# Loading the first indices ahead of x on one DMA queue, in a max-unpool kernel

## Chip, cores, metric

One Trainium2 chip, one core of it. The time is the device time of one execution in microseconds; medians are given with the lowest and highest run.

## The reference

Each value of `x` goes to one of the four places of a 2x2 block of the output, chosen by an index from 0 to 3; the other three places are zero.

```python
def setup_inputs():
    batch, channels, h, w = 16, 64, 32, 32
    return {"x": np.random.randn(batch, channels, h, w).astype(np.float32),
            "indices": np.random.randint(0, 4, (batch, channels, h, w)).astype(np.int32),
            "kernel_size": 2}

# for every b, c, i, j:
idx = indices[b, c, i, j]
output[b, c, 2 * i + idx // 2, 2 * j + idx % 2] = x[b, c, i, j]
```

On the device `x` has 4 MiB, the indices, which arrive as 64-bit integers, 8 MiB, and the output 16 MiB.

## The kernel before

There are 1024 images of 32x32, eight on each of 128 partitions. Everything is loaded by three transfers on the Sync queue: all of x, the indices of the first three images (`FIRST = 3`), the other five. VectorE writes, for each of the four places, `(index == place) * x`, two images per operation, or one at the border between the two loads of indices. Two images make a group, and each of the four groups is stored by one transfer of 4 MiB. The fourth group reuses the first output buffer. A semaphore is a counter on which an engine waits: each load raises its own by 16, one for each of the 16 DMA engines that carry it, and has landed with the last of these increments.

```python
    cut = FIRST * 2 * N
    with Program(nc) as program:        # puts the loads at the head of the Sync queue
        program.first(nc.sync.dma_start(out=x_t, in_=x_v).then_inc(x_in, 16))
        for half, part in enumerate((slice(0, cut), slice(cut, None))):
            program.first(
                nc.sync.dma_start(out=idx_t[:, part], in_=idx_v[:, part]).then_inc(
                    idx_in[half], 16))

        nc.vector.wait_ge(x_in, 16).then_inc(x_in, -16)
        for t in range(T):
            g, k = t // G, t % G
            if t in (0, FIRST):
                half = int(t == FIRST)
                nc.vector.wait_ge(idx_in[half], 16).then_inc(idx_in[half], -16)
            # ... (n is 1 or 2 images)
            for pidx in range(4):
                op = nc.vector.scalar_tensor_tensor(
                    out=o_c[:, k : k + n, :, pidx // 2, :, pidx % 2],
                    in0=idx_c[:, t : t + n], scalar=pidx, in1=x_c[:, t : t + n],
                    op0=mybir.AluOpType.is_equal, op1=mybir.AluOpType.mult)
            if k + n == G:
                op.then_inc(made, 1)

        for g in range(NG):
            nc.sync.wait_ge(made, g + 1)
            nc.sync.dma_start(out=out_v[g], in_=out_t[g]).then_inc(
                stored if g else stored_0, 16)
        # ... (wait for the last stores)
```

Of the kernel before, what the change touches and what calls it, by code (L numbers as in the profile page):

```python
# [1 line left out]

# [4 lines left out]

P = 128
F32 = mybir.dt.float32
I32 = mybir.dt.int32  # L10


class Program:



    def __init__(self, nc):
        self.nc = nc
        self.block = nc.main_func.blocks[0]
        self.kernel_block = nc.cur_bb.bb.name  # L20
        self.moved = 0

    def __enter__(self):
        ins = self.block.instructions
        self.branches = [i for i in ins if "Branch" in type(i).__name__]
        n = len(ins) - len(self.branches)
        assert all("Branch" in type(ins[k]).__name__ for k in range(n, len(ins)))
        del ins[n:]
        self.nc.switch_bb(self.block.name, parent=None)
        self.symbolic = self.nc._always_lower_symbolic_ap  # L30
        self.nc._always_lower_symbolic_ap = False
        return self

    def first(self, made):
        ins = self.block.instructions
        assert ins[len(ins) - 1].name == made.ins.name
        moved = ins.pop()
        at = next(k for k, i in enumerate(ins) if i.engine == moved.engine)
        ins.insert(at + self.moved, moved)
        self.moved += 1  # L40

    def last(self, made):


        def move(nc):
            ins = self.block.instructions
            at = next(k for k, i in enumerate(ins) if i.name == made.ins.name)
            nc.main_func.blocks[-1].instructions.append(ins.pop(at))

        self.nc.at_finalize(move)  # L50

    def __exit__(self, kind, *_):
        self.nc._always_lower_symbolic_ap = self.symbolic
        if kind is None:
            for b in self.branches:
                self.block.instructions.append(b)
            self.nc.switch_bb(self.kernel_block, parent=None)


@with_exitstack  # L60
def kernel(
    ctx: ExitStack,
    tc: tile.TileContext,
    x: bass.AP,
    indices: bass.AP,
    kernel_size: bass.AP,
    out: bass.AP,
):
    nc = tc.nc
    assert kernel_size == 2  # L70

    B, C, H, W = x.shape
    n_img = B * C
    T = n_img // P
    assert T * P == n_img and C % T == 0

    G = 2
    NG = T // G
    FIRST = 3
    N = H * W  # L80
    x_v = x.rearrange("b (ch t) h w -> (b ch) (t h w)", t=T)
    idx_v = indices.rearrange("b (ch t) h w -> (b ch) (t h w)", t=T).bitcast(I32)
    out_v = out.rearrange("b (ch g t) oh ow -> g (b ch) (t oh ow)", g=NG, t=G)

    x_t = nc.alloc_sbuf_tensor("x_t", [P, T * N], F32).ap()
    idx_t = nc.alloc_sbuf_tensor("idx_t", [P, T * 2 * N], I32).ap()
    out_t = [
        nc.alloc_sbuf_tensor(f"out_t{g}", [P, G * 4 * N], F32).ap()
        for g in range(NG - 1)
    ]  # L90
    out_t.append(out_t[0])

    x_in = nc.alloc_semaphore("x_in")
    idx_in = [nc.alloc_semaphore(f"idx_in{g}") for g in range(2)]
    made = nc.alloc_semaphore("made")
    stored_0 = nc.alloc_semaphore("stored_0")
    stored = nc.alloc_semaphore("stored")

    x_c = x_t.rearrange("p (t i j) -> p t i j", t=T, j=W)
    idx_c = idx_t.rearrange("p (t i j two) -> p t i j two", t=T, j=W, two=2)[  # L100
        :, :, :, :, 0
    ]
    cut = FIRST * 2 * N

    with Program(nc) as program:
        program.first(nc.sync.dma_start(out=x_t, in_=x_v).then_inc(x_in, 16))
        for half, part in enumerate((slice(0, cut), slice(cut, None))):
            program.first(
                nc.sync.dma_start(out=idx_t[:, part], in_=idx_v[:, part]).then_inc(
                    idx_in[half], 16  # L110
                )
            )

        nc.vector.wait_ge(x_in, 16).then_inc(x_in, -16)
        for t in range(T):
# [5 lines that stand above are left out]
            if k == 1 and t != FIRST:  # L121
                continue
            n = 1 if k == 1 or t + 1 == FIRST else 2
            if g == NG - 1:
                nc.vector.wait_ge(stored_0, 16).then_inc(stored_0, -16)
            o_c = out_t[g].rearrange(
                "p (m i two j wo) -> p m i two j wo", m=G, two=2, wo=2, j=W
# [4 lines that stand above are left out]
                    in0=idx_c[:, t : t + n],  # L132
                    scalar=pidx,
                    in1=x_c[:, t : t + n],
                    op0=mybir.AluOpType.is_equal,
                    op1=mybir.AluOpType.mult,
# [7 lines that stand above are left out]
                stored if g else stored_0, 16  # L144
            )
        nc.sync.sem_inc(made, -NG)
        program.last(
            nc.sync.wait_ge(stored, 16 * (NG - 1)).then_inc(stored, -16 * (NG - 1))
        )


# [1 line left out]
_INS = ['x', 'indices', 'kernel_size']  # L153
_OUTS = [((16, 64, 64, 64), 'float32')]

_NUMBERS = {'kernel_size': 2}


# [26 lines left out]
```

## Time and profile before

| | before |
|---|---|
| median of the first three runs | 71.57 us (71.49 to 71.67) |
| span of the profiled run | 70.5 us |
| VectorE | 35.6 us busy, from 19.81 to 55.40 without a gap |
| DMA queue | 97.4% of 16 engines' span |
| landings | x 12.4, first indices 19.6, other indices 31.8 us |

In the profile DVE is VectorE, POOL is GpSimd, PE is TensorE and SP is the Sync engine; a name with q, such as SPq, is the engine's own instruction queue. The stores and loads are issued on SPq and carried by the DMA engines. A wait is put down to the semaphore instruction that held it, so "DVEq L119" is VectorE's own queue waiting at line 119. The prediction below shows the lines.

### The profile page before, as it was taken

How to read it: one execution, taken by the hardware profiler on the slowest of the kernel's cores; microseconds unless marked ns; L12 is line 12 of the kernel's file. 1: busy time of each engine (PE TensorE's matmuls, PEld its weight loads, DVE VectorE, ACT ScalarE, POOL GpSimd, SP SyncE). 2: the span in 40 equal slices, each digit the busy share in tenths (PEclk: the TensorE clock that was granted, in tenths of full speed). 3: DMA queues.
4: the chain of work that ended last, by engine and by line, in shares of the span. 5: the costliest groups of instructions: out<-in, count | busy, mean ns of one | idle time of the engine just before them, and what ended most of it. 6: DMA issues, size and time to landing. Idle time of an engine off the chain costs nothing.

```text
span 70.5 us, 72 instructions
## 1 busy us (share of the span) xinstructions
DVE 35.6 (50%) x20; POOL 0.2 (0%) x4
## 2 busy tenths in 40 slices
DVE  0000000000079999999999999999999400000000
POOL 1000000000000000000000000000000000000000
DMA  9779798899988999969899997979798999979790
GB/s 260 316 316 558 335 558 344 376 432 446 595 372 372 395 511 535 418 298 521 372 428 465 409 483 335 539 316 558 335 521 372 446 446 409 483 335 539 316 558 37
DMA packets 1008, 29.36 MB, mean 416 GB/s; under 512 B 112, under 2 KB 112, under 8 KB 112
## 3 DMA queue, kind: packets, MB, share of 16 engines
q1 hardware_dynamic: 1008, 29.36, 97.4%
HBM read 12.58 MB, written 16.78 MB: 416 GB/s over the span
## 4 chain that ended last, share of the span: by engine, by line
DVE 46%; DVEq 4%; issue 1%
DVE out_t L130 46%; DVEq L180 4%
## 5 line engine op out<-in xcount | busy, mean ns | idle before, releaser
L130 DVE SCALAR_TENSOR_TENSOR out_t<-idx_t,x_t 128x2048 f32<-128x2048 int32 (+1 forms) x20 | 35.6, 1857 | 19.8 <-DVEq L119 19.8
L166 POOL MEMSET const-uint8-127<- 128x1 uint8 x1 | 0.1, 103 | 0.0
L166 POOL MEMSET const-bfloat16-1.0<- 128x1 bf16 x1 | 0.1, 102 | 0.0
L166 POOL MEMSET const-float32-0.0<- 128x1 f32 x1 | 0.1, 99 | 0.2 <-issue 0.2
L166 POOL MEMSET const-float32-1.0<- 128x1 f32 x1 | 0.1, 99 | 0.0
## 6 DMA issues: line engine op xcount, KB each, us to landing
out_dram<-out_t SPq DMA_DIRECT2D x4, 4096.0 KB, 13.8
idx_t<-in_indices_dram SPq DMA_DIRECT2D x1, 5120.0 KB, 30.9
x_t<-in_x_dram SPq DMA_DIRECT2D x1, 4096.0 KB, 12.4
idx_t<-in_indices_dram SPq DMA_DIRECT2D x1, 3072.0 KB, 19.2
```

Of the source, the lines that this page charges most:

```text
L130: op = nc.vector.scalar_tensor_tensor(out=o_c[:, k : k + n, :, pidx // 2, :, pidx % 2], in0=idx_c[:, t : t + n], scalar=pidx, in1=x_c[:, t ...
L166: nc = _bacc.Bacc("TRN2", target_bir_lowering=False, num_devices=1)
L180: with _tile.TileContext(nc) as tc:
```

## The change

The loads are issued in another order: first indices, x, other indices. The apparent aim is to have the indices that VectorE needs first in place early. The helper that puts loads at the head of the queue also changes its rule, from "count what I moved" to "in front of the queue's first drain", which comes to the same place.

```diff
-        at = next(k for k, i in enumerate(ins) if i.engine == moved.engine)
-        ins.insert(at + self.moved, moved)
-        self.moved += 1
+        at = next(k for k, i in enumerate(ins)
+                  if i.engine == moved.engine and isinstance(i, mybir.InstDrain))
+        ins.insert(at, moved)
 ...
+        program.first(nc.sync.dma_start(out=idx_t[:, :cut], in_=idx_v[:, :cut])
+                      .then_inc(idx_in[0], 16))
         program.first(nc.sync.dma_start(out=x_t, in_=x_v).then_inc(x_in, 16))
-        for half, part in enumerate((slice(0, cut), slice(cut, None))):
-            program.first(nc.sync.dma_start(out=idx_t[:, part], in_=idx_v[:, part])
-                          .then_inc(idx_in[half], 16))
+        program.first(nc.sync.dma_start(out=idx_t[:, cut:], in_=idx_v[:, cut:])
+                      .then_inc(idx_in[1], 16))
```

(Line breaks shortened, the rest unchanged.)

More of the change, by code (lines that the diff above doesn't have):

```diff
@@ L20, in __init__ @@
         self.kernel_block = nc.cur_bb.bb.name
-        self.moved = 0
     def __enter__(self):
@@ L37, in first @@
         moved = ins.pop()
-        at = next(k for k, i in enumerate(ins) if i.engine == moved.engine)
-        ins.insert(at + self.moved, moved)
-        self.moved += 1
+        at = next(
+            k
+            for k, i in enumerate(ins)
+            if i.engine == moved.engine and isinstance(i, mybir.InstDrain)
+        )
+        ins.insert(at, moved)
     def last(self, made):
@@ L105 @@
     with Program(nc) as program:
-        program.first(nc.sync.dma_start(out=x_t, in_=x_v).then_inc(x_in, 16))
-        for half, part in enumerate((slice(0, cut), slice(cut, None))):
-            program.first(
-                nc.sync.dma_start(out=idx_t[:, part], in_=idx_v[:, part]).then_inc(
-                    idx_in[half], 16
-                )
+        program.first(
+            nc.sync.dma_start(out=idx_t[:, :cut], in_=idx_v[:, :cut]).then_inc(
+                idx_in[0], 16
+            )
+        )
+        program.first(nc.sync.dma_start(out=x_t, in_=x_v).then_inc(x_in, 16))
+        program.first(
+            nc.sync.dma_start(out=idx_t[:, cut:], in_=idx_v[:, cut:]).then_inc(
+                idx_in[1], 16
             )
+        )
         nc.vector.wait_ge(x_in, 16).then_inc(x_in, -16)
```

## The prediction

> **What bounds the kernel now.** I read the page's head first (busy shares, slices, queues), then the waits, then the issues with their landings, then the timeline, and last a table of stretches that follows the stages those views gave.
>
> The page's busy shares and its DMA lines:
>
> ```profile
> DVE 35.6 (50%) x20; POOL 0.2 (0%) x4
> ...
> DVE  0000000000079999999999999999999400000000
> ...
> DMA  9779798899988999969899997979798999979790
> ...
> q1 hardware_dynamic: 1008, 29.36, 97.4%
> HBM read 12.58 MB, written 16.78 MB: 416 GB/s over the span
> ```
>
> VectorE, the only engine that computes, works 35.6 of 70.5 us, in one block in the middle. The transfers fill 97.4% of what 16 DMA engines could do in the span, in every slice from the first to the last but one. The page's chain of waits ("DVE 46%") starts at a VectorE wait and puts the rest on VectorE; it doesn't follow transfers, so by itself it would point at the wrong resource.
>
> The waits of VectorE, and of the queue that issues:
>
> ```profile
> DVE out_t L130 <- DVEq L119: 19.8, 1, 19.8
> ...
> SPq L143 <- DVE out_t L130: 52.7, 4, 27.0
> SPq L148 <- SPq L148: 14.0, 1, 14.0
> ```
>
> VectorE waits once, 19.8 us, at line 119, for the first load of the indices; afterwards never. The queue waits for VectorE before each of four stores, and 14.0 us at the end for the last store to land.
>
> The page's issues (the last column is issue to landing), and the timeline:
>
> ```profile
> out_dram<-out_t SPq DMA_DIRECT2D x4, 4096.0 KB, 13.8
> idx_t<-in_indices_dram SPq DMA_DIRECT2D x1, 5120.0 KB, 30.9
> x_t<-in_x_dram SPq DMA_DIRECT2D x1, 4096.0 KB, 12.4
> idx_t<-in_indices_dram SPq DMA_DIRECT2D x1, 3072.0 KB, 19.2
> ...
> 0.00 0.38 SPq L106 DMA_DIRECT2D x_t<-in_x_dram  x1
> ...
> 0.43 0.90 SPq L109 DMA_DIRECT2D idx_t<-in_indices_dram  x2
> 19.81 35.59 DVE L130 SCALAR_TENSOR_TENSOR out_t<-idx_t,x_t 128x2048 f32<-128x2048 int32 x20 [19.81 <-DVEq L119]
> 28.73 27.03 SPq L143 DMA_DIRECT2D out_dram<-out_t  x4
> ```
>
> x lands at 12.4, the first indices at 0.43 + 19.2 = 19.6, the other indices at 0.90 + 30.9 = 31.8. VectorE starts 0.2 after the second landing, runs without a gap from 19.81 to 55.40, and the first store is issued at 28.73, when the last indices still have 3 us to go.
>
> The table of stretches (length; busy time of DVE and POOL; clock; DMA share; GB/s):
>
> ```profile
> 0.00:2.00 2.00, 0.00 (x0) 0.20 (x4) 1.00 0.89 246
> 2.00:4.00 2.00, 0.00 (x0) 0.00 (x0) 1.00 0.64 279
> 4.00:12.00 8.00, 0.00 (x0) 0.00 (x0) 1.00 1.02 439
> 12.00:20.00 8.00, 0.19 (x1) 0.00 (x0) 1.00 1.00 429
> 20.00:31.00 11.00, 11.00 (x7) 0.00 (x0) 1.00 1.03 444
> 31.00:41.00 10.00, 10.00 (x8) 0.00 (x0) 1.00 1.02 439
> ```
>
> From 4 us on the rate is 430 to 440 GB/s whichever tensor moves and whichever way. Only the first 4 us are poorer. The transfers bound the time from end to end; VectorE is hidden behind them, as long as it never lets the queue run dry.
>
> The records of single packets in the trace make this exact. Each engine moves eight packets per transfer, one packet per partition row: 1.213 us for 32 KB (x, stores), 0.912 for 24 KB (first indices), 1.514 for 40 KB (other indices), each next one starting as the one before ends. Chained together, the 56 data packets of every engine have no gap over 0.004 us between any two. The first packets begin between 1.01 and 2.35 us. The engine that begins last also ends last: it starts at 2.35, ends x at 12.02, first indices at 19.30, other indices at 31.39, last store at 70.11. So the end is that engine's start plus 67.76 us of packets, plus 0.39 for the last landing and the end of the span.
>
> **What the Trainium skill says.** "DMA: Bandwidth & Descriptors", section "Where 436 GB/s comes from", gives 16 ports x 256 bits x 850 MHz = 435.2 GB/s as the ceiling of a core's transfers. The trace agrees: 32,768 bytes in 1.213 us on 16 engines is 432 GB/s. The same page, "Queues, rings and completion order", has each DMA engine take its descriptors in ring order, with the semaphore written only after that engine's data. The landings (x, first indices, other indices, in order of issue) agree. And "Why a DMA increments its semaphore by 16 and not by 1" says that only the full 16 means all data has landed; so a wait ends with the slowest of 16 engines. Here the 16 increments of a load are spread over 0.7 us, and VectorE starts after the last. "Perfetto Trace Analysis", section "Summary: the profiler window per engine type", says the interval of such an issue leaves out the movement of data: 0.38 us against 12.4 to landing here. So I judge the loads by landings and packets, not by the 0.38.
>
> **The change part by part.** The comparison of instruction orders shows equal lists on every engine but for one swap: the queue now has first indices, x, other indices, where it had x, first indices, other indices. The new rule for where a load is inserted (before the engine's first drain, not at its first instruction) comes to the same place: in both programs the three loads head the issuing engine's list. No byte, packet, wait, or VectorE instruction is added or removed.
>
> 1. Issue. A load of indices takes 0.425 to 0.432 us to issue, x takes 0.383 (the durations of the issues at lines 109 and 106). With the indices in front, the first packet may come 0.04 us later than its 1.01 now. On the path: +0.04.
>
> 2. First indices and x. In either order the two take 8 x 0.912 + 8 x 1.213 = 17.0 us of each engine. On the last engine they take 19.30 - 2.35 = 16.95, the records overlapping by a few ns. What precedes is start-up: 2.35 us from the first issue to that engine's first packet. On most other engines the first packet begins before 1.3 and takes 1.76 to 2.17 us instead of 1.21; the three that begin at 1.41, 1.81 and 2.35 take 1.54, 1.48 and 1.21, so all first packets end between 2.9 and 3.6, and all later ones take their normal time. That looks like a delay that each engine pays once, not like a rate in proportion to size, so I let it stand with 24 KB in front: +0.00.
>
> 3. The landing that VectorE needs. It needs both loads. Now it waits for x until 12.4 and for the first indices until 19.67 (last of 16 increments). Afterwards the indices land at about 2.35 + 8 x 0.91 + 0.37 = 10.0 (0.37 being the time from the last packet's end to its increment, 19.67 - 19.30) and x, 4,096 KB behind 3,072 KB, at 19.7. The wait that lasts changes its name, not its end. The code waits for x first and indices second, so after the x wait ends, one satisfied wait stands between it and the first operation: 0.02 us of its own, with its dispatch perhaps 0.05 to 0.1. VectorE starts at 19.8 to 19.95 and ends at 55.4 to 55.55, with 35.6 us of work as now.
>
> 4. What a late VectorE costs. The first store is issued at 28.73. From issue to first packet takes about 1.0 us (x: 0.00 to 1.01), so its packets could start at 29.74; the first engine is free at 30.71. The slack is 0.97. If the last engine's first packet comes 2.35 after every issue, not only after the first of all, that engine could start at 31.08 and is free at 31.39: slack 0.31. The next issues, at 37.81, 46.62 and 55.43, meet packets that start at 40.39, 50.07 and 59.75: slacks of 1.6, 2.4 and 3.3. A delay of 0.15 fits in the smallest: +0.00. The reused first output buffer is no obstacle either: its store lands at 41.52, and the last group begins at 46.51.
>
> 5. The rest, other indices and stores, is the same series of packets: 70.11 - 19.30 = 50.8 us.
>
> Sum: 71.57 + 0.04 = 71.61, so 71.6.
>
> **The rivals.** One: VectorE starts earlier, since indices come first. That is the apparent aim of such a change, and it would hold if the first operations needed little of x. Against it: line 119's wait shows VectorE starting after all 7,168 KB have landed, x is still one load with one wait, and even an earlier VectorE could not help, since the stores would queue behind the last indices on engines that are already full. Time: unchanged.
>
> Two: the start-up shrinks with the first packet. If the slow first packets are slow in proportion to size, 24 KB rather than 32 KB saves a quarter of the excess, (2.17 - 1.21) / 4, about 0.25: 71.3. For it: they are by far the slowest packets. Against it: the engine that ends last had no slow packet at all, it only began late; it gains nothing unless it begins earlier.
>
> Three: the start-up grows. Rows of indices lie 64 KB apart in memory, each load of them taking a part; rows of x are contiguous. If cold reads of spread rows are slower, or the last engine is served later behind a longer issue, 0.2 to 0.4 is lost: 71.9. Warm reads speak against it: 24 KB in 0.912 us is 26.9 GB/s for an engine, and x's 1.213 is 27.0.
>
> Four: the queue runs dry before the first store because VectorE is late. By step 4 it takes between 0.31 and 0.97 us of delay before anything is lost; nothing in the change makes more than 0.15. If it did, say 1.5 us late, the time would be 72.1.
>
> **Range and chances.** The three runs before spread from 71.49 to 71.67, about 0.1 either way. Start-up is the one term with an open sign, -0.3 to +0.3. That gives 71.3 to 71.9. Two per cent is 1.43 us, more than the whole start-up loss, and steady transfer can't be shortened without fewer bytes: faster 0.01. A loss of that size would need rival four with at least 1.7 us of delay (0.31 + 1.43): slower 0.02. Within 2%: 0.97.
>
> **What would show it right or wrong.** In the issues, first indices landing near 9 to 10 us and x at about 19 to 20 us after issue, other indices 30.9 as now. In the waits, the 19.8 us of VectorE stays within 0.2, now ended by x's landing. The queue's share stays near 97%, the stretches from 4 us on near 430 to 440 GB/s, and the wait for the last store near 14.0. A DMA share well under 0.9 in a stretch around 30 us would mean that the stores came late; other indices landing over 0.3 away from 31.8 would mean that start-up has changed; a VectorE start far from 19.8 would break step 3; a store or load at a lower steady rate would break step 5, and then the prediction as a whole.

## The result

| | before | changed |
|---|---|---|
| median, six runs each | 71.62 us (71.49 to 71.75) | 71.47 us (71.41 to 71.79) |
| ratio | | 0.9989, 95% interval 0.9968 to 1.0011 |

A ratio is the mean time of one kernel's fast runs over that of the other's in the same rounds, so not quite the ratio of the medians. Within 2%, and inside the predicted 71.3 to 71.9.

The page of the changed kernel, busy shares and transfers:

```profile
DVE 35.6 (51%) x20; POOL 0.2 (0%) x4
...
DMA  8799997979988999869898999989898989999891
...
q1 hardware_dynamic: 1008, 29.36, 97.4%
```

Its issues (KB, then us from issue to landing) and its timeline:

```profile
out_dram<-out_t SPq DMA_DIRECT2D x4, 4096.0 KB, 13.8
idx_t<-in_indices_dram SPq DMA_DIRECT2D x1, 5120.0 KB, 30.8
x_t<-in_x_dram SPq DMA_DIRECT2D x1, 4096.0 KB, 19.0
idx_t<-in_indices_dram SPq DMA_DIRECT2D x1, 3072.0 KB, 9.7
...
0.00 0.38 SPq L110 DMA_DIRECT2D idx_t<-in_indices_dram  x1
...
0.43 0.42 SPq L114 DMA_DIRECT2D x_t<-in_x_dram  x1
...
19.67 35.60 DVE L137 SCALAR_TENSOR_TENSOR out_t<-idx_t,x_t 128x2048 f32<-128x2048 int32 x20 [19.67 <-DVEq L126]
28.60 27.03 SPq L150 DMA_DIRECT2D out_dram<-out_t  x4
```

Look at the landings, not at VectorE: the first indices are there at 9.7 instead of 19.6 us, x at 19.4 instead of 12.4. VectorE needs both and so starts at 19.67 where it started at 19.81. The wait changed its cause and kept its end; the queue's share is the same 97.4%.

The waits of VectorE and the last one of the queue:

```profile
DVE out_t L137 <- DVEq L126: 19.7, 1, 19.7
...
SPq L155 <- SPq L155: 14.1, 1, 14.1
```

"L126" is the wait for the first indices, though they had landed 10 us before: it is the second of two waits in a row, and the first, for x, let it through only at 19.45 (the semaphore instruction at line 121). The view names the wait instruction nearest to the operation, not the late transfer. The landings name it.

### The profile page after: what moved, and what is told of

Its sections match the earlier page's. It is cut to its first block, busy times and chain, and to the rows that moved or that the text cites. A ratio compares the mean times of both kernels' runs of the same rounds, so it can differ in the third digit from the quotient of the medians.

```text
span 70.5 us, 72 instructions
## 1 busy us (share of the span) xinstructions
DVE 35.6 (51%) x20; POOL 0.2 (0%) x4
## 3 DMA queue, kind: packets, MB, share of 16 engines
q1 hardware_dynamic: 1008, 29.36, 97.4%
## 4 chain that ended last, share of the span: by engine, by line
DVE 46%; DVEq 4%; issue 1%
DVE out_t L137 46%; DVEq L187 4%
```

## Experiments

Eleven runs were made, one of them of the changed kernel again; the edits below are edits of the changed kernel. Below, A is the theory of the prediction: the packets on the 16 DMA engines bound the time from end to end. B is the rival that the chain of waits suggests: first load, then VectorE, then last store. C came up after the first four runs. Packets are read from the trace's record of single packets. "Effective start" is worked out for each engine: the start of its first packet after 5 us, less what all its earlier bytes would take at the steady rate. All ratios are to the kernel before, run on the same chip, so a run's gain or loss contains the 0.1 to 0.3 us that the changed order itself saves (see after_again). The jobs ran on different chips, so ratios of different jobs are compared only roughly.

### VectorE earlier: e1_split

```diff
-  load indices 0-2;  x 0-7;  indices 3-7
+  load indices 0-2;  x 0-2;  x 3-7;  indices 3-5;  indices 6-7
   # each with its own semaphore, waited for where it is first needed
```

> x and the indices are split in order of need (indices 0-2, x 0-2, x 3-7, indices 3-5, indices 6-7), same bytes, same queue. Both theories: VectorE needs only 4.7 MB before its first operation, which land at about 2.4 + 10.9 + 0.4 = 13.7 us instead of 19.5, and it then runs its 35.6 us almost without a wait, to about 49.3. Theory A (the engines' packets bound the time end to end): the stores still queue behind the last indices, whose last packet ends near 31.4; time 71.5, plus or minus 0.2, wait for the last store 20 us instead of 14. Theory B (the path is first load, VectorE, last store): 6 us are saved, 65.5.

Measured: 72.79 us (72.64 to 72.91), ratio 1.0144 (1.0115 to 1.0173). VectorE did start 6 us earlier, and the first store was issued at 22.32 instead of 28.60:

```profile
13.40 26.84 DVE L145 SCALAR_TENSOR_TENSOR out_t<-idx_t,x_t 128x2048 f32<-128x2048 int32 x16 [13.40 <-DVEq L130]
22.32 29.60 SPq L158 DMA_DIRECT2D out_dram<-out_t  x4
```

B is dead: 6 us earlier in, nothing gained. But A isn't whole either; it said 71.5, and the kernel lost 1.1 us against before. The packets tell where. All loads ran at their normal pace until 28.5 us. Then the last three packets of each engine (16 KB, normally 0.611 us) took up to 1.28, and the stores began at 31.8 to 32.5 instead of 30.7 to 31.4. From there on everything was steady again.

### Fewer bytes: e2_less and e3_split_less

```diff
-  load indices 3-7                     # e2; in e3 the split loads of e1 without the last
+  load indices 3-5
-  in0=idx_c[:, t : t + n]
+  in0=idx_c[:, t % 6 : t % 6 + n]      # wrong result for images 6 and 7, on purpose
```

> 2.1 MB of indices (images 6 and 7) are not loaded and the last group uses images 0 and 1 again: a wrong result on purpose. VectorE's start and work stay. Theory A counted naively: 2.1 MB at 432 GB/s are 4.85 us, 66.6. Theory A with the slack of my prediction: the loads end near 26.55, but the first store is issued only at 28.6 and its first packets come at 29.6 or later, so only the slack is won, 0.97 us (70.5) if all engines start promptly, down to 0.3 (71.2) if one starts as late as at the start of the program; the engines idle about 3 us before the first store. Theory B: unchanged, 71.5.

> Both of the above: loads split in order of need, and 2.1 MB less (wrong result on purpose). Now VectorE starts at about 13.7, its first group is done by 22.6, before the loads end at about 26.5, so nothing hides the bytes saved. Theory A: 71.5 - 4.85 = 66.6, share of the queue again near 97%. Theory B: as e1, 65.5, with no difference between e1 and e3.

e2: 70.10 us (70.04 to 70.15), ratio 0.9769. A hole opens in the transfers, two slices (of 1.7 us) at zero, while the first store waits for VectorE, issued at 28.44:

```profile
DMA  8699998897999980097978979798797977979793
...
28.44 27.03 SPq L151 DMA_DIRECT2D out_dram<-out_t  x4
```

In the packets each engine idles 3.1 to 3.6 us, and all sixteen begin the store between 29.28 and 29.44, 0.8 to 1.0 us after its issue. So the gain against before was 1.6 us, not the 4.85 of the bytes and not nothing, and more than the 0.3 to 1.0 that I expected: here no engine begins its store late, as some began the first load, so the slack of the engine that ends last is 31.39 - 29.7 = 1.7 us. The cautious branch of the prediction's step 4 (slack 0.31) was wrong.

e3: 67.91 us, ratio 0.9465. Against e1, which differs only in those bytes, that is 72.79 - 67.91 = 4.88 us, and 2.1 MB at 432 GB/s are 4.85. Where nothing hides them, bytes cost what A says. The level is 1.3 us too high for A, as with e1: the last two load packets of each engine (24 KB, normally 0.912) took up to 1.78.

### VectorE later: e4_late and e5_late_small

```diff
+  nc.vector.scalar_tensor_tensor(out=scratch[:, :NN], in0=x_t[:, :NN], scalar=0.0,
+      in1=x_t[:, :NN], op0=is_equal, op1=mult)   # once, before the first operation
   # NN = 2048 in e4, 256 in e5
```

> One extra VectorE operation on 2048 elements into a scratch tile before the first: VectorE is 2.2 us later, all else equal. Theory A: the first store is issued at 30.8, its packets start at about 31.8 on engines that are free between 30.6 and 31.4, so 0.4 to 0.7 us are lost on the engine that ends last (72.0 to 72.2), and up to 1.8 if an engine starts its store late again (73.3). A gap of 0.4 to 1.3 us shows in each engine's packets before the first store and nowhere else. Theory B: the full 2.2 us, 73.7.

> The changed kernel with one dummy VectorE operation on 256 elements, 0.33 us, in front. Theory A with its slack (at least 0.31 us, by e2 and e4 nearer 1 us): no loss, 0.995 to 0.997 of before as the changed kernel, or 0.1 us less where a few last packets no longer meet the first store. Theory B: 0.33 us more than the changed kernel, 1.000 to 1.001 of before.

e4: 72.35 us (72.19 to 72.41), ratio 1.0080 (1.0053 to 1.0107), so 2.2 us of delay cost 0.6 against before; a little above the 72.0 to 72.2 of A, far from B's 73.7. The gap before the first store is 0.51 to 1.05 us in the packets, and no gap elsewhere exceeds 0.03.

e5: 71.54 us, ratio 0.9983 (0.9971 to 0.9994). The delay was 0.35 us (19.50 to 19.85), and nothing is lost to be seen against before. The ratio lies between the 0.995 to 0.997 expected of A and the 1.000 to 1.001 expected of B, and both lie just outside its interval. So this run separates nothing; e4 does that.

### The order again: after_again

> The changed kernel once more, for a sharper ratio to the kernel before on one chip. Theory A (only start-up can differ): ratio between 0.996 and 1.004. A rival with start-up in proportion to the first packet's size: 0.25 us less, ratio 0.9965.

71.47 us (71.39 to 71.60) against 71.79 (71.66 to 71.97), ratio 0.9961 (0.9947 to 0.9975). With the first 0.9989, the change saves something like 0.1 to 0.3 us. That is real on this chip. It fits the rival with start-up in proportion to size (0.9965) as well as A; e7 and e10 below decide that. It isn't VectorE's doing, for 6 us there gained nothing (e1). The span was 70.1 us; the changed kernel's first profile, 70.5, fell on its slowest run (71.79).

### Why the split lost: e8_split_late and e9_early_store

Theory C: a store that stands queued behind a load that is still running slows the end of that load. In e1 the store was queued 9 us before the engines were free; in both original kernels only 2.

```diff
 # e8: e1, and before the first operation
+  three dummy VectorE operations of 2.2 us, into scratch
 # e9: the changed kernel, whole loads, and
-  nc.vector.wait_ge(x_in, 16)          # before the first operation
+  if t == 2: nc.vector.wait_ge(x_in, 16)
-  in1=x_c[:, t : t + n]
+  in1=(x_c if t else idx_c)[:, t : t + n]    # wrong result for the first group, on purpose
```

> The split loads of e1, but three dummy VectorE operations of 2.2 us in front, so that the first store is issued at about 29 us as in the changed kernel and not at 22.3. Theory C (in e1 the last 48 KB per engine of the loads ran at about half rate because a store already stood queued behind them): the loss of 1.1 us goes away, 71.5 to 71.8, and the last 16 KB packets take 0.61 us again. Rival D (five smaller loads cost more than three): 72.8 as e1.

> The changed kernel with its three whole loads, but the first group takes the indices in place of x (a wrong result on purpose), so VectorE starts after the first load, at about 9.8 us, and the first store is issued at about 18.9 while the last load still has 12 us to go. Theory C: the last 40 KB packet or two of each engine slow down as in e1, the time is 0.8 to 1.3 us above the changed kernel, 72.4 to 72.8. Rival D: 71.5, like the changed kernel, for the loads are the same.

e8: 71.55 us (71.54 to 71.62), ratio 0.9972. The split alone costs nothing. e9: 72.93 us (72.89 to 73.05), ratio 1.0164, a little beyond the expected range. It has the loads of the changed kernel and the loss of e1. The first store's issue in e8, then in e9, where VectorE's later pause shows too:

```profile
28.98 27.03 SPq L168 DMA_DIRECT2D out_dram<-out_t  x4
```

```profile
18.72 36.83 SPq L151 DMA_DIRECT2D out_dram<-out_t  x4
19.50 4.63 DVE L138 SCALAR_TENSOR_TENSOR out_t<-idx_t,x_t 128x1024 f32<-128x1024 int32 x4 [0.80 <-DVEq L124]
32.94 22.25 DVE L138 SCALAR_TENSOR_TENSOR out_t<-idx_t,x_t 128x1024 f32<-128x1024 int32 x12 [8.81 <-DVEq L127]
```

Rates around the change from loads to stores. Columns are stretch, length, busy VectorE and GpSimd, clock, DMA share, GB/s. A packet's bytes count where it ends, so a short stretch swings by a packet per engine. First before, then e1, e8, e9:

```profile
20.00:28.00 8.00, 8.00 (x4) 0.00 (x0) 1.00 1.06 461
28.00:32.00 4.00, 4.00 (x4) 0.00 (x0) 1.00 0.94 406
```

```profile
20.00:28.00 8.00, 8.00 (x8) 0.00 (x0) 1.00 0.99 426
28.00:32.00 4.00, 4.00 (x5) 0.00 (x0) 1.00 0.98 303
```

```profile
20.00:28.00 8.00, 8.00 (x5) 0.00 (x0) 1.00 0.99 426
28.00:32.00 4.00, 4.00 (x4) 0.00 (x0) 1.00 1.00 426
```

```profile
20.00:28.00 8.00, 4.13 (x4) 0.00 (x0) 1.00 1.12 481
28.00:32.00 4.00, 0.00 (x0) 0.00 (x0) 1.00 0.79 215
```

Compare e1 with e8: the same five loads, 303 and 426 GB/s, and the store issued at 22.32 and 28.98. In e1 the DMA engines are busy (0.98) and slow: this is no gap, it is long packets. In e9 VectorE does nothing between 24.1 and 32.9 us (its busy time is 0.00), so it isn't VectorE's writes that slow the loads; each engine's last packet of 40 KB took 2.43 to 2.82 us instead of 1.51. C holds in both directions, D (more loads cost more) in neither. The store had stood queued since 18.72, yet in e9 the packets are slow only from 27.5 on, and only the last one or two of each engine; in e1 the last three. What inside a DMA engine does this, no run shows, and a store issued early on another queue than the loads was not tried.

### The start: e6_two_queues, e7_tiny_first, e10_x24_first

```diff
 # e6
-  nc.sync.dma_start(x);   nc.sync.dma_start(indices 3-7)
+  nc.scalar.dma_start(x); nc.scalar.dma_start(indices 3-7)
 # e7
-  load indices 0-2
+  load indices 0; load indices 1-2
 # e10
-  load indices 0-2;  x 0-7;  indices 3-7
+  load x 0-5;  indices 0-2;  x 6-7;  indices 3-7     # and one dummy operation of 2.2 us
```

> The first indices stay on the Sync queue, x and then the other indices go to the Scalar queue, so both first loads are issued at 0 us. Bytes and the order of need are the same; the first indices and x now land together near 19.5. Theory A: only start-up can change; 71.2 to 71.6. If the late first packet of some engines comes from one queue being served engine by engine, it shrinks: first packets of all engines begin before 1.6 us and 0.3 us are saved. If two queues make each engine switch at a cost: 0.3 to 1 us slower.

> The first load of the indices is cut into image 0 (8 KB rows) and images 1 and 2 (16 KB rows); everything else as in the changed kernel. If the start-up excess is in proportion to the first packet's size (0.24 us for 8 KB less, from before to after), 16 KB less gives another 0.4 to 0.5 us: ratio to before 0.989 to 0.991. If the excess is a fixed delay by now, as after: 0.996. If the extra load costs issue time: 0.997 to 1.000.

> Six images of x first, again 24 KB a row, then three of the indices, two of x, the rest of the indices; a dummy VectorE operation of 2.2 us keeps the first store at about 28.4 us. If the 0.3 us of after come from the smaller first packet: 0.995 to 0.997 of before, as after. If they come from the indices being the first tensor read: 1.000.

| kernel | first packet | effective start, mean of 16 engines | ratio |
|---|---|---|---|
| before | x, 32 KB | 1.92 us | 1 |
| e10_x24_first | x, 24 KB | 2.00 us | 1.0009 (0.9996 to 1.0023) |
| changed, two profiles | indices, 24 KB | 1.75 and 1.72 us | 0.9989 and 0.9961 |
| e7_tiny_first | indices, 8 KB | 1.72 us | 0.9986 (0.9973 to 0.9998) |
| e6_two_queues | indices, 24 KB, and x | 1.78 us | 0.9990 (0.9966 to 1.0014) |

All eleven profiles of kernels that read the indices first lie between 1.72 and 1.78 us; the two that read x first lie at 1.92 and 2.00. The engine that starts last, which sets the end where all later packets are regular, shows the same: about 2.3 us in both profiles with x first, 1.8 to 2.1 in the others. The size of the first packet doesn't matter: 8 KB gave what 24 KB gave, where proportion would have given a ratio of 0.989 to 0.991, and x in 24 KB gave what x in 32 KB gave. By its ratio alone e7 would also fit its third branch (an extra load costs issue time, 0.997 to 1.000); its start does not differ. The second queue of e6 brought nothing: its median, 71.70 us, lies a little above the 71.2 to 71.6 expected, and the latest of the engines' first packets began at 1.68 us, not before 1.6. So what the changed order saves, about 0.2 us, comes with the tensor that is read first. Why x starts more slowly than the indices (rows 32 KB apart, those of the indices 64, and other addresses) stays open, and with two profiles on the x side it isn't more than an observation.

None of these versions beats the changed kernel beyond doubt: e8 on its chip had 0.9972 beside 0.9961, and e5 and e7 ran on another chip.

## Why the prediction was right, point by point

- **The bound** (read from the queue's share and the packets without gaps): right. e1 takes 6 us from VectorE's start and gains nothing; e3 against e1 gives the bytes' cost as 4.88 us for a computed 4.85. The 430 to 440 GB/s "from 4 us on" were stated too narrowly: the rows of that view that the prediction left out have 417 to 433, and the changed kernel's have 397 to 455. The packets' own times are steadier.
- **Step 1, issue, +0.04**: wrong in sense, harmless in size. The first issue took 0.38 us with the indices in front as well; the longer 0.42 belongs to the second and third place in the queue.
- **Step 2, the start, +0.00**: mis-sized by about -0.2 us (mean effective start 1.92 to 1.75 and 1.72). I had let the start-up stand and kept "proportional to size" as a rival that lands at 71.3. The time came out between the two, but e7 shows that this rival's reason is wrong too. Rival three, a longer start with the indices in front, had the sign the other way round. The prediction's own sign of a changed start, other indices over 0.3 us away from 31.8, stayed out in the first profile (31.7) and came in after_again (31.4).
- **Step 3, VectorE's start 19.8 to 19.95**: it was 19.67, because the loads ended earlier (last increment of x at 19.42 where that of the indices had been at 19.67), and 19.47 in after_again. The cost of the extra, already satisfied wait was estimated well: from last increment to first operation 0.25 us instead of 0.14.
- **Step 4, slack**: a delay is free up to about a microsecond, as said, and on the engine that ends last up to 1.7 (e2). The branch with 0.31 fell. What the step lacks is the other side: it treats an early store as free, and so does rival one ("could not help"). It hurts by 1.1 us and more (e1, e9).
- **Step 5, the rest is one series of packets**: right but for the changeover. The wait for the last store was 14.0 and 14.1 us, and the last packet ended at 70.11 in both first profiles, but that equality is luck. In the changed kernel's first profile, its slowest run, four of the last 40 KB load packets took 1.56 to 1.92 us instead of 1.51; the engine that ended last had one of 1.76 and so lost 0.25 us, about what the earlier start had gained. In the profile of before none was slow, in after_again one (1.79). It looks like C on a small scale (first store issued at 28.60); whether it is, no run tests.

The sum of 71.6 stands 0.13 above the measured 71.47. Steps 1 and 2 together (0.04 and about 0.2) would put it 0.24 too high; the 0.1 between is within the spread of the runs and is not assigned.

## What to carry to other kernels

Where an operation waits for several loads, their order on one queue changes which of them it waits for; what counts is when the last of them is in (19.67 us before, 19.42 changed). In this kernel, with the DMA engines busy from end to end, it was bytes (e3), the start (x or indices first), a dry queue (e4) and the changeover from loads to stores (e1, e9) that moved the time, and a compute engine that started earlier even lost by queueing a store too soon behind loads. Read landings and packets before believing the chain of waits: it named VectorE, and a VectorE that started 6 us earlier made the kernel slower.

## What the Trainium skill lacked or had wrong

- "DMA: Bandwidth & Descriptors", section "Rules for kernel authors", advises to issue a transfer early and wait for it late. It doesn't say that a store issued early behind loads on the same queue slows their last packets: 40 KB in 2.43 to 2.82 us instead of 1.51 (e9), 1.1 us on the kernel against before (e1 and e9 alike).
- The same page, section "Latency and other measured facts", gives about 600 ns to the first byte for this kind of issue. From the start of the first issue to the first packet it was 1.01 us here, from the issue's end 0.63; the page doesn't say from where it counts. For a store into idle engines it was 0.8 to 1.0 from the issue's start (e2).
- No page has the start-up of the single engines: the first packet of most engines took 0.3 to 1.0 us longer than a later one of its size, whatever its size (8 KB: up to 1.04 instead of 0.31; 32 KB: up to 2.17 instead of 1.21), and the whole start was 0.2 us longer with x first.
